# Strassen's seven products for the up projection of a hybrid decoder trunk, with block sums of its weights made by GpSimd

## The chip, the core and the metric

The kernel runs on one core of a Trainium2 chip. The metric is device time in microseconds (us) of one execution. Engines: TensorE (PE: matmuls, PEld: its weight loads), VectorE (DVE), ScalarE (ACT), GpSimd (POOL) and SyncE (SP, which issues most DMAs). Every engine runs its own instructions strictly in the order in which they stand in its queue.

## The reference

One layer on 2048 prompt tokens and 8 × 8 sample tokens, in float32, width 1024:

```python
h = rmsnorm(x, norm1_g)
q, ka, va, rw, gates = split(h @ w_in)              # 1024 x 4608
att = windowed_attention(q, ka, va, ...)
rw_out = rwkv7_mixer(rw, ...)
g_a, g_b = split(sigmoid(gates))
x = x + (g_a * (att @ w_pa) + g_b * (rw_out @ w_pb)) @ w_o
# conv_ffn(rmsnorm(x, norm2_g)):
ug, uv = split(h2 @ w_up)                           # 1024 x 2 * 2816
c = conv_b + sum_j conv_w[j] * shift(ug, j)         # causal, width 3
x = x + (gelu(c) * uv) @ w_down                     # 2816 x 1024
y = rmsnorm(x, final_g)
```

## The kernel before

Every large product takes three matmuls for each tile of 128 rows of the contraction: weights and activations are split into a high part (ACT rounds, `whi`, `A`/`B` first tile) and a low part (a subtraction, `wlo`), and hi·hi, hi·lo, lo·hi are added in PSUM. Activations lie with features on the partitions and tokens along the free axis.

**Phase 1** has six groups of 256 to 384 tokens. Each multiplies by the 36 tiles of `w_in` (1024 x 128 each) while attention and RWKV work of the same and of the previous group runs between the products; the order on PE is written out by hand (`ordered`, with the times `Y_...` at which each piece is taken). The rows of a raw product go through ACT into `raw`; POOL copies its last column into `carry` for the next group (line 624), and POOL also does `BK` (982, 983), `sp` (1166), `Y` (1274) and the scaling by the norm (532, 539). In the first three groups 72 weight tiles are split; their parts are written to memory and read back by the other groups.

**Phase 2** has three groups of 704 tokens, held as two halves of 352: `w_ab` (8 tiles of 1024 x 128), `w_o` (8), then the 22 f tiles of the up product, each once for `w_ug` and once for `w_uv`, in four parts of 6, 6, 6 and 4 f tiles, each part followed by its share of `w_down` (8 tiles). A weight tile of 8 x 128 columns serves 48 matmuls of 352 columns. It is split in two halves of 512 columns; `W_POOL = (2, 0)` gives every second half's subtraction to POOL, the other to DVE (`wsub`, line 424). The norm's factor `rs` isn't in the operand of the up product: the operand is x2 times the weight vector (line 1323, `A`), and `rs` is multiplied in where the products leave PSUM (1427) and on POOL (1449). So the up products need not wait for the norm. Behind each up product stand the width-3 convolution (1431, 1437), GELU (1445 to 1448) and, when the gate product is there, 1456 and the split of the result into `B` (1323).

## Time and profile before

| | |
|---|---|
| median of 3 runs | 3415.2 us (3404.68 to 3422.92) |
| profiled execution | 3414.19 us, span 3412.4 us |
| granted clock, mean | 0.975 |
| busy: PE | 3274.9 us (96%), 23574 matmuls |
| busy: DVE | 1941.7 us (57%) |
| busy: ACT | 1162.7 us (34%) |
| busy: POOL | 1106.6 us (32%) |

Busy time counts an engine's own instructions; neighbouring ones overlap a little, so the duration of one is longer than its share of a dense stretch. Phase 1 ends at about 1465 us.

### The profile page before, as it was taken

How to read it: one execution, taken by the hardware profiler on the slowest of the kernel's cores; microseconds unless marked ns; L12 is line 12 of the kernel's file. 1: busy time of each engine (PE TensorE's matmuls, PEld its weight loads, DVE VectorE, ACT ScalarE, POOL GpSimd, SP SyncE). 2: the span in 40 equal slices, each digit the busy share in tenths (PEclk: the TensorE clock that was granted, in tenths of full speed). 3: DMA queues.
4: the chain of work that ended last, by engine and by line, in shares of the span. 5: the costliest groups of instructions: out<-in, count | busy, mean ns of one | idle time of the engine just before them, and what ended most of it. 6: DMA issues, size and time to landing. Idle time of an engine off the chain costs nothing.

```text
span 3412.4 us, 59346 instructions
## 1 busy us (share of the span) xinstructions
PE 3274.9 (96%) x23574; PEld 3124.1 (92%) x23574; DVE 1941.7 (57%) x3658; ACT 1162.7 (34%) x2370; POOL 1106.6 (32%) x1242
## 2 busy tenths in 40 slices
PE   7899999989999999899999999999999999999998
PEld 6879888878888889799999999999999999999998
DVE  6764775664664765655454465555464655564564
ACT  4444443332333333223232233332232323232232
POOL 4333432321221222152233332423243342343342
PEclk9989989899999999999999999999999999999999
DMA  5446467684565658562222224512222352222222
GB/s 174 147 142 228 162 204 240 214 267 151 195 197 191 211 181 287 170 217 68 64 70 72 67 63 130 172 59 77 70 66 72 97 181 74 63 70 73 68 69 74
DMA packets 197069, 460.22 MB, mean 135 GB/s; under 512 B 62719, under 2 KB 95111, under 8 KB 196791
## 3 DMA queue, kind: packets, MB, share of 16 engines
q1 hardware_dynamic: 169367, 396.33, 36.0%
q0 software_dynamic: 8704, 37.78, 3.3%
q10 hardware_dynamic: 18720, 22.31, 1.8%
q8 instruction: 185, 3.03, 0.4%
...
HBM read 377.03 MB, written 79.31 MB: 134 GB/s over the span
## 4 chain that ended last, share of the span: by engine, by line
PE 78%; DVE 9%; DMA 6%; ACT 3%; issue 2%; POOL 2%; SPq 0%; ACTq 0%; DVEq 0%; POOLq 0%
PE acc L287 69%; PE ps L287 5%; DMA w<-w_in 2%; PE psA L287 2%; DVE LN L1034 1%; DVE TX L1032 1%; POOL wlo L424 1%; ACT whi L383 1%; PE psY L287 1%; ACT at L778 1%; DMA gates<-raw 1%; POOL th L1386 1%; DVE wlo L424 1%; DVE at L768 0%; DMA raw<-x 0%
## 5 line engine op out<-in xcount | busy, mean ns | idle before, releaser
L287 PE MATMUL acc<-A,whi 128*128 128x352 f32 x4992 | 1008.6, 323 | 3.8 <-DVE A L1320 3.1
L287 PE MATMUL acc<-h,whi 128*128 128x384 f32 (+2 forms) x3456 | 899.2, 340 | 14.3 <-DVE h L588 4.1
L287 PEld LDWEIGHTS acc<-A,whi 128*128 128x128 f32 x4992 | 837.3, 188 | 5.4 <-DVE A L1320 4.0
L424 POOL TENSOR_TENSOR wlo<-w,whi 128x512 fp32r<-128x512 f32 (+2 forms) x347 | 477.2, 1376 | 1070.4 <-ACT whi L383 977.9
L383 ACT CAST whi<-w 128x512 fp32r<-128x512 f32 (+2 forms) x696 | 373.6, 581 | 1066.9 <-PE acc L287 496.9
L287 PEld LDWEIGHTS acc<-h,whi 128*128 128x128 f32 x3456 | 621.8, 194 | 47.0 <-issue 15.1
L287 PE MATMUL acc<-A,wlo 128*128 128x352 f32 x2496 | 605.7, 324 | 0.0
L287 PE MATMUL acc<-B,whi 128*128 128x352 f32 x2880 | 582.5, 323 | 4.6 <-ACT B L1322 2.4
L287 PE MATMUL acc<-h,wlo 128*128 128x384 f32 (+2 forms) x1728 | 581.0, 336 | 1.4 <-DMA wlo<-w_in_lo 1.0
L287 PEld LDWEIGHTS acc<-B,whi 128*128 128x128 f32 x2880 | 481.9, 188 | 6.4 <-DVE B L1323 3.3
L424 DVE TENSOR_TENSOR wlo<-w,whi 128x512 fp32r<-128x512 f32 (+2 forms) x349 | 302.8, 868 | 256.8 <-ACT whi L383 244.4
L287 PEld LDWEIGHTS acc<-A,wlo 128*128 128x128 f32 x2496 | 435.4, 188 | 0.1
L287 PE MATMUL acc<-B,wlo 128*128 128x352 f32 x1440 | 350.2, 323 | 0.0
L287 PEld LDWEIGHTS acc<-h,wlo 128*128 128x128 f32 x1728 | 334.3, 193 | 15.0 <-issue 3.6
L287 PEld LDWEIGHTS acc<-B,wlo 128*128 128x128 f32 x1440 | 250.9, 188 | 0.0
L1478 DVE TENSOR_TENSOR x<-x,acc 128x352 f32<-128x352 f32 x188 | 89.3, 516 | 227.2 <-PE acc L287 227.2
L1449 POOL TENSOR_TENSOR ss<-ss,ssq 128x704 f32<-128x704 f32 x66 | 113.2, 1715 | 297.2 <-DVE ss L1448 264.0
L1437 DVE SCALAR_TENSOR_TENSOR cc<-ub,vt,cc 128x704 f32<-128x704 f32 (+1 forms) x132 | 145.9, 1105 | 37.4 <-ACT cc L1431 35.6
L1427 DVE TENSOR_TENSOR ub<-acc,ssq 128x352 f32<-128x352 f32 (+1 forms) x132 | 61.5, 507 | 117.5 <-PE acc L287 116.2
L1323 DVE SCALAR_TENSOR_TENSOR B<-ss,B 128x704 fp32r<-128x704 f32 x66 | 113.4, 1718 | 4.0 <-ACT B L1322 3.9
L1445 ACT ACTIVATE ss<-cc 128x704 f32<-128x704 f32 x66 | 52.4, 793 | 162.4 <-DVE cc L1437 110.5
L619 ACT COPY raw<-acc 128x384 f32<-128x384 f32 (+1 forms) x84 | 37.4, 445 | 168.4 <-PE acc L287 164.1
...
## 6 DMA issues: line engine op xcount, KB each, us to landing
whi<-w_in_hi SPq DMA_DIRECT2D x144, 512.0 KB, 4.6
wlo<-w_in_lo SPq DMA_DIRECT2D x144, 512.0 KB, 3.9
w<-w_in SPq DMA_DIRECT2D x72, 512.0 KB, 4.5
w<-w_ug SPq DMA_DIRECT2D x66, 512.0 KB, 3.5
w<-w_uv SPq DMA_DIRECT2D x66, 512.0 KB, 3.5
...
w_in_hi<-whi SPq DMA_DIRECT2D x36, 512.0 KB, 2.7
w_in_lo<-wlo SPq DMA_DIRECT2D x36, 512.0 KB, 5.3
```

The costliest lines, as they stand in the source:

```text
L287: self.pe(self.nc.tensor.matmul(out, lhsT, rhs, start=start, stop=stop), max(n * (1 if rhs.dtype == F32R else 4) / 2.4, 25))
L383: nc.scalar.copy(out=hi[:, a:b], in_=w[:, a:b])
L424: i = eng.tensor_tensor(**kw)
L619: nc.scalar.copy(out=raw[:, 1:1 + n], in_=acc[:, :n])
L778: nc.scalar.activation(out=t[:, h, :], in_=t[:, h, :], func=AF.Exp, bias=nm[:, h:h + 1], accum_out=su[:, h:h + 1])
L1032: nc.vector.tensor_tensor(out=tv, in0=LN[:NL, j:j + 1, j + 1:32].broadcast_to([NL, j, w]), in1=LN[:NL, 0:j, j:j + 1].broadcast_to([NL, j, ...
L1323: nc.vector.scalar_tensor_tensor(out=lo[:, :T], in0=src[:, :T], scalar=scale, in1=hi[:, :T].bitcast(F32), op0=MUL, op1=SUB)
L1427: nc.vector.tensor_tensor(out=ub[:, 2 + a:2 + e], in0=pp[:, :e - a], in1=rs[:, a:e], op=MUL)
L1437: nc.vector.scalar_tensor_tensor(out=cc[:, :n], in0=ub[:, j:j + n], scalar=self.v(wn, f), in1=cc[:, :n], op0=MUL, op1=ADD)
L1445: nc.scalar.activation(out=s[:, :T], in_=cc[:, :T], func=AF.Square, scale=GELU_A)
L1449: nc.gpsimd.tensor_tensor(out=s[:, :T], in0=s[:, :T], in1=rs[:, :T], op=MUL)
L1478: nc.vector.tensor_tensor(out=x2[m][:, a:b], in0=x2[m][:, a:b], in1=pp[:, :b - a], op=ADD)
```

## The change

**Up product.** Tokens are taken as two halves and the contraction as two halves of 512, and two neighbouring f tiles as the two halves of the output: a 2 x 2 by 2 x 2 block product in seven block products (Winograd's form) instead of eight. A run is one pair of f tiles of `w_ug` or of `w_uv`; a block product is 4 x 128 rows by 128 columns by 352 tokens, 12 matmuls. Two block products share one weight tile ("chunk", 24 matmuls). The results are combined as they leave PSUM (`product`: line 1473 `u`, 1476 `u3`, 1466; `put` of the up run, 1646, and of the gate run, 1662 and 1663).

**Operands.** The norm is now multiplied into x2 before the up product (`scaled`, line 1564); four sums of activation blocks are made (`second_chunk`, 1680 to 1690) and all seven operands are split (1334). `w_o` is run once for each token half, so its tiles are loaded and split twice; the norm of the first half is made inside the second run of `w_o`. In the first part of a group the block products 1 and 2 of all six runs stand ahead of the others; they need only the first half's operands.

**Weight sums.** Four sums of the four blocks of each weight pair are made once, on POOL, by `weight_sums`, spawned in phase 1: 88 times two loads of 128 KB, four subtractions or additions of 128x128 and one store of 256 KB, 23 MB read and 23 MB written in all. Two buffers `ws` serve it.

**Weights of phase 2** come as one stream in the order of use: loaded three tiles ahead and split one ahead (`next_w2`), with seven slots for raw, high and low tiles. `W_POOL` is set so that every subtraction of a split is DVE's, in phase 1 too. Outside a stretch from the end of `w_o` to the tenth chunk, PE's order in phase 2 is no longer written by hand.

```diff
-W_POOL = (2, 0)
+W_POOL = (1 << 30, 0)
...
+            self.sums_d = [[self.dram.tile([128, 4, 4, 128], F32, name=f"sums{x}{i}") for i in range(cfg.ff // 2)] for x in "gv"]
...
+            self.spawn(self.weight_sums())
...
-            self.bufs = dict(A=16, B=16, x2=8, th=4, tm=2, ub=2, cc=2, ss=2, ssq=1, carry=2, nrm=3)
+            self.bufs = dict(A=56, B=12, x2=8, th=4, ub=2, cc=2, ss=4, u=6, u3=1, ug=1, ssq=1, carry=2, nrm=3)
...
+            self.ordered = False
+            self.worder2, self.at2, self.nload2, self.nsplit2, self.raw2, self.split2 = self.weight_order(), 0, 0, 0, [], []
...
+    def weight_sums(self):
+        nc = self.nc
+        yield Y_weight_sums_1
+        last = None
+        for i in range(self.cfg.ff // 2):
+            for x, wn in enumerate(("w_ug", "w_uv")):
+                for k in range(4):
+                    v = self.t("ws", [128, 4, 128])
+                    for j in range(2):
+                        nc.gpsimd.dma_start(out=v[:, 2 * j:2 * j + 2], in_=self.A[wn][2 * i + j][:, k::4])
+                    if last:
+                        nc.gpsimd.dma_start(out=last[0], in_=last[1])
+                    yield Y_weight_sums_2
+                    a11, a12, a21, a22 = (v[:, j] for j in range(4))
+                    for o, p, q, op in ((a22, a21, a22, ADD), (a21, a11, a21, SUB), (a11, a22, a11, SUB), (a12, a12, a11, SUB)):
+                        nc.gpsimd.tensor_tensor(out=o, in0=p, in1=q, op=op)
+                    last = self.sums_d[x][i][:, :, k], v
+                    yield Y_weight_sums_2
+        nc.gpsimd.dma_start(out=last[0], in_=last[1])
...
+    REST = (6, 7, 5, 4, 3)
+    def part_chunks(self, part):
+        runs = [(0, part[0] // 2)]
+        for i, f in enumerate(part):
+            runs += [(0, u // 2) for u in part[i + 1:i + 2]] + [(1, f // 2)]
+        if part[0] == 0:
+            seq = [(*r, p) for r in runs for p in (1, 2)] + [(*r, p) for r in runs for p in self.REST]
+        else:
+            seq = [(*r, p) for r in runs for p in (1, 2) + self.REST]
+        return runs, [seq[i:i + 2] for i in range(0, len(seq), 2)]
...
+    def next_w2(self, *what):
+        order = self.worder2
+        while self.nload2 < min(self.at2 + 4, len(order)):
+            spec = order[self.nload2]
+            w = self.wtile("w", F32)
+            if isinstance(spec[0], str):
+                name, m, a, b = spec
+                kt = b - a
+                self.nc.sync.dma_start(out=w[:, :kt], in_=self.A[name][m][:, a:b])
+            else:
+                kt = 4 * len(spec)
+                for j, (x, i, p) in enumerate(spec):
+                    self.nc.sync.dma_start(out=w[:, j * 4:j * 4 + 4], in_=self.block_src(x, i, self.PRODUCTS[p][1]))
+            self.raw2.append((w, kt, None))
+            self.nload2 += 1
+        while self.nsplit2 < min(self.at2 + 2, len(order)):
+            self.split2.append(self.split_w(self.raw2.pop(0)))
+            self.nsplit2 += 1
+        assert order[self.at2] == what, (order[self.at2], what)
+        self.at2 += 1
+        return self.split2.pop(0)
...
+    def block_product(self, wt, k0, xs):
+        (hi, lo), w, o = wt, self.cfg.tmax2 // 2, self.pt("acc")[:, :self.cfg.tmax2 // 2]
+        for k in range(4):
+            xh, xl = xs[k]
+            for i in range(3):
+                self.mm(o, (hi, hi, lo)[i][:, k0 + k, :], (xh, xl, xh)[i], k == 0 and i == 0, k == 3 and i == 2)
+        return o
+    PRODUCTS = {1: ("b11", "a11"), 2: ("b21", "a12"), 3: ("b22", "s4"), 4: ("t4", "a22"), 5: ("t1", "s1"), 6: ("t2", "s2"), 7: ("t3", "s3")}
...
+    def product(self, R, p, wt, k0):
+        nc, w = self.nc, self.cfg.tmax2 // 2
+        o = self.block_product(wt, k0, R.ops[self.PRODUCTS[p][0]])
+        def five():
+            R.put(1, 1, R.u3, R.p5)
+            nc.vector.tensor_tensor(out=R.u, in0=R.p5, in1=R.u, op=ADD)
+        if p == 1:
+            R.u = self.t("u", [128, w])
+            nc.scalar.copy(out=R.u, in_=o)
+        elif p == 2:
+            R.put(0, 0, R.u, o)
+        elif p == 6:
+            nc.vector.tensor_tensor(out=R.u, in0=o, in1=R.u, op=ADD)
+        elif p == 7:
+            R.u3 = self.t("u3", [128, w])
+            nc.vector.tensor_tensor(out=R.u3, in0=o, in1=R.u, op=ADD)
+            if R.p5 is not None:
+                five()
+        elif p == 5:
+            R.p5 = o
+            if R.u3 is not None:
+                five()
+        elif p == 4:
+            R.put(1, 0, R.u3, o)
+        else:
+            R.put(0, 1, R.u, o)
+    def run_products(self, chunk, runs):
+        wt = self.next_w2(*chunk)
+        for k, (x, i, p) in enumerate(chunk):
+            R = runs[x, i]
+            if p > 2 and R.hold:
+                R.hold = False
+                for z in R.held:
+                    R.put(*z)
+            self.product(R, p, wt, k * 4)
 
...
-            h2.append(self.split(x, "A", T, self.v("n2", m)))
...
+        def norm(c):
+            (a, b), more = chunks[c], [lastsq]
+            yield from self.rstd_steps(rs[:, a:b], b - a, "acc", more)
+        def scaled(dst, m, c):
+            a, b = chunks[c]
+            nc.vector.scalar_tensor_tensor(out=dst, in0=x2[m][:, a:b], scalar=self.v("n2", m), in1=rs[:, a:b], op0=MUL, op1=MUL)
+        def first_chunk():
+            for j in range(4):
+                h = self.t("ss", [128, TM])
+                h1.append(h)
+                for i, n in ((0, "b11"), (1, "b21")):
+                    d = h[:, i * w:i * w + w]
+                    scaled(d, i * 4 + j, 0)
+                    ops[n][j] = self.split_half(d)
+        for c, (a, b) in enumerate(chunks):
+            for m in range(8):
+                hi, lo = self.next_w2("w_o", m, 0, 8)
+                if c == 1 and m == 7:
+                    self.ordered, self.last_pe = True, None
+                pp, = self.gemm2(hi, lo, mix, (c,))
+                x = x2[m]
+                if c == 0:
+                    nc.gpsimd.dma_start(out=x[:, :T], in_=A["x"][m][:, c0:c1])
+                nc.vector.scalar_tensor_tensor(out=x[:, a:b], in0=pp[:, :w], scalar=0.5, in1=x[:, a:b], op0=MUL, op1=ADD)
+                if m < 7:
+                    self.sumsq(rs, x, m, a, b)
+                else:
+                    lastsq = self.t("cc", [128, TM])[:, a:b]
+                    nc.scalar.activation(out=lastsq, in_=x[:, a:b], func=AF.Square)
+                if c == 1 and m == 1:
+                    for _ in norm(0):
+                        pass
+                    first_chunk()
+        norm1 = norm(1)
...
-            nc.gpsimd.tensor_tensor(out=s[:, :T], in0=s[:, :T], in1=rs[:, :T], op=MUL)
...
+        def gate(f, ss, acts):
+            done, out = [0, 0], [None, None]
+            def put(row, c, s, ps):
+                a, b = chunks[c]
+                x = ss[row][:, a:b]
+                t = self.t("ug", [128, w])
+                nc.vector.tensor_tensor(out=t, in0=ps, in1=s, op=ADD)
+                nc.vector.tensor_tensor(out=x, in0=x, in1=t, op=MUL)
+                done[row] += 1
+                if done[row] == 2:
+                    out[row] = self.split(ss[row], "B", T)
+                    if None not in out:
+                        acts.extend(lambda c, h=h: [z[:, c * w:c * w + w] for z in h] for h in out)
+            return Run(1, f // 2, put)
+        h2 = [None] * 4
+        def second_chunk(stage):
+            for j in range(4):
+                if stage == 0:
+                    h2[j] = self.t("th", [128, TM])
+                p, q, r, s = h1[j][:, :w], h1[j][:, w:T], h2[j][:, :w], h2[j][:, w:T]
+                if stage == 0:
+                    scaled(r, j, 1)
+                    nc.vector.tensor_tensor(out=p, in0=r, in1=p, op=SUB)
+                    ops["t1"][j] = self.split_half(p)
+                elif stage == 1:
+                    scaled(s, 4 + j, 1)
+                    nc.vector.tensor_tensor(out=p, in0=s, in1=p, op=SUB)
+                    ops["t2"][j] = self.split_half(p)
+                elif stage == 2:
+                    nc.vector.tensor_tensor(out=r, in0=s, in1=r, op=SUB)
+                    ops["t3"][j] = self.split_half(r)
+                elif stage == 3:
+                    nc.vector.tensor_tensor(out=q, in0=q, in1=p, op=SUB)
+                    ops["t4"][j] = self.split_half(q)
+                else:
+                    ops["b22"][j] = self.split_half(s)
 
...
+            order, todo = self.part_chunks(part)
+            runs = {}
             for f in part:
-                s = up(f)
-                if pend is not None:
-                    acts.append(gate(*pend))
-                pend = (f, s)
-            acts.append(gate(*pend))
+                runs[0, f // 2], o = up(f)
+                runs[1, f // 2] = gate(f, o, acts)
+            if part[0] == 0:
+                for r in order[1:]:
+                    runs[r].hold = True
+            for i, chunk in enumerate(todo):
+                if part[0] == 0:
+                    if i in (1, 2):
+                        next(norm1, None)
+                    if 2 <= i < 7:
+                        second_chunk(i - 2)
+                    if i == 9:
+                        self.ordered = False
+                self.run_products(chunk, runs)
...
```

Counts by the code: the up product has 44 tiles x 48 = 2112 matmuls in a group before, and 11 pairs x 2 runs x 7 x 12 = 1848 after. Tiles split in a group of phase 2: 92 before, 8 + 16 + 77 + 32 = 133 after.

On POOL's queue, in phase 1's first group, before: one subtraction of a weight split between the copies that end a raw tile (`raw`, `carry`).

```order
L624 COPY carry_233<-raw_768 128x1
L424 TENSOR_TENSOR wlo_780<-w_775,whi_779 128x512
L621 MEMSET raw_929 128x1
L624 COPY carry_233<-raw_833 128x1
L424 TENSOR_TENSOR wlo_843<-w_840,whi_842 128x512
L952 COPY PC_443<-t_P_878 128x6
L983 TENSOR_TENSOR BK_910<-xk_772,t_sw_874 64x6x64 x2
L621 MEMSET raw_971 128x1
```

After, at the same place in the first group:

```order
L1385 TENSOR_TENSOR ws_4592<-ws_4592 128x128 x4
L1379 DMA ws_4723<-w_ug 128x2x128 x2
L1381 DMA sumsg2_104<-ws_4592 512x1x128
L627 COPY carry_255<-raw_855 128x1
L624 MEMSET raw_951 128x1
L1385 TENSOR_TENSOR ws_4723<-ws_4723 128x128 x4
L1379 DMA ws_4901<-w_ug 128x2x128 x2
L1381 DMA sumsg2_104<-ws_4723 512x1x128
L956 COPY PC_465<-t_P_900 128x6
```

The splits are gone from POOL, and weight sums stand between the same copies. Read along the whole queue, 25 of the 88 stores of sums stand ahead of the fourteenth `COPY carry` of the first group (the last raw tile of its RWKV rows), 57 ahead of its first `Y`, and all 88 ahead of the second tile's `BK` of the second group.

On DVE's queue, at the norm of a group's second half (before: the norm of the whole group, ahead of the first up results, first token group), before:

```order
L436 SCALAR_TENSOR_TENSOR nrm_17366<-nrm_17366,nrm_17364 128x6
L437 SCALAR_TENSOR_TENSOR nrm_17365<-nrm_17366,nrm_17365 128x6
L452 MEMSET nrm_21924 128x1
L424 TENSOR_TENSOR wlo_17572<-w_17569,whi_17571 128x512
L1427 TENSOR_TENSOR ub_17417<-acc_17334,ssq_16772 128x352
L1427 TENSOR_TENSOR ub_17417<-acc_17335,ssq_16772 128x352
L1437 SCALAR_TENSOR_TENSOR cc_17418<-ub_17417,vt_90,cc_17418 128x704 x2
L1446 SCALAR_TENSOR_TENSOR ss_17426<-ss_17426,cc_17418 128x704
L1448 SCALAR_TENSOR_TENSOR ss_17426<-ss_17426,cc_17418 128x704
```

After, where the second half's norm is in (second token group; `wlo_24718` is the low part of the chunk that PE takes next):

```order
L426 TENSOR_TENSOR wlo_24718<-w_24582,whi_24717 128x512 x2
L1564 SCALAR_TENSOR_TENSOR th_24686<-x2_23904,vt_90,ssq_23903 128x352
L1564 SCALAR_TENSOR_TENSOR th_24693<-x2_23905,vt_90,ssq_23903 128x352
L1680 TENSOR_TENSOR ss_24313<-th_24686,ss_24313 128x352
L1680 TENSOR_TENSOR ss_24324<-th_24693,ss_24324 128x352
L1564 SCALAR_TENSOR_TENSOR th_24700<-x2_23906,vt_90,ssq_23903 128x352
L1334 TENSOR_TENSOR A_24690<-ss_24313,A_24689 128x352
L1680 TENSOR_TENSOR ss_24335<-th_24700,ss_24335 128x352
L1334 TENSOR_TENSOR A_24697<-ss_24324,A_24696 128x352
L1564 SCALAR_TENSOR_TENSOR th_24707<-x2_23907,vt_90,ssq_23903 128x352
L1564 SCALAR_TENSOR_TENSOR th_24686<-x2_23908,vt_90,ssq_23903 128x352
L1334 TENSOR_TENSOR A_24704<-ss_24335,A_24703 128x352
```

Before, a split and the first results follow the norm at once. After, 21 instructions of 352 columns (12 of them shown) stand between the split of one chunk (`wlo_24718`) and that of the next (`wlo_24779`).

On DVE's queue among the up products, before (one f tile of up and one of gate):

```order
L1427 TENSOR_TENSOR ub_17627<-acc_17577,ssq_16772 128x352
L1427 TENSOR_TENSOR ub_17627<-acc_17578,ssq_16772 128x352
L424 TENSOR_TENSOR wlo_17782<-w_17779,whi_17781 128x512
L1437 SCALAR_TENSOR_TENSOR cc_17628<-ub_17627,vt_90,cc_17628 128x704 x2
L1446 SCALAR_TENSOR_TENSOR ss_17636<-ss_17636,cc_17628 128x704
L1448 SCALAR_TENSOR_TENSOR ss_17636<-ss_17636,cc_17628 128x704
L1456 TENSOR_TENSOR ss_17499<-ss_17499,acc_17650 128x352
L1456 TENSOR_TENSOR ss_17499<-ss_17499,acc_17651 128x352
L424 TENSOR_TENSOR wlo_17846<-w_17843,whi_17845 128x512
L1323 SCALAR_TENSOR_TENSOR B_17703<-ss_17499,B_17702 128x704
```

After, a place in the first part of the second token group (two chunks):

```order
L426 TENSOR_TENSOR wlo_24984<-w_24889,whi_24983 128x512 x2
L1646 TENSOR_TENSOR ub_25002<-acc_24989,u3_24978 128x352
L1466 TENSOR_TENSOR u_24604<-acc_24989,u_24604 128x352
L1662 TENSOR_TENSOR ug_25188<-acc_24738,u_24736 128x352
L1646 TENSOR_TENSOR ub_25002<-acc_25005,u3_24978 128x352
L426 TENSOR_TENSOR wlo_25034<-w_24942,whi_25033 128x512 x2
L1623 SCALAR_TENSOR_TENSOR cc_25019<-ub_25002,vt_90,cc_25019 128x704
L1646 TENSOR_TENSOR ub_24619<-acc_25039,u_24604 128x352
L1623 SCALAR_TENSOR_TENSOR cc_25019<-ub_25002,vt_90,cc_25019 128x704
L1646 TENSOR_TENSOR ub_25064<-acc_24668,u_24666 128x352
L1623 SCALAR_TENSOR_TENSOR cc_25053<-ub_24619,vt_90,cc_25053 128x704
L1632 SCALAR_TENSOR_TENSOR ss_25025<-ss_25025,cc_25019 128x704
```

Before, one half of a split stands among four or five instructions; after, both halves (`x2`), and each block product that leaves PSUM brings one addition or two, ahead of the same convolution and GELU (1623, 1632).

## Rows read from the trace of the kernel before

**Rows 1.** Busy time of each engine in phase 1 and phase 2 (stretches; x: instructions that started).

```profile
core 0: us, PE busy (x) PEld busy (x) DVE busy (x) ACT busy (x) POOL busy (x), PEclk, DMA share, GB/s
0.00:1465.00 1465.00, 1354.91 (x11631) 1208.38 (x11632) 905.10 (x2165) 562.28 (x1407) 435.60 (x611) 0.95 0.60 198
1465.00:3412.00 1947.00, 1919.96 (x11945) 1915.73 (x11944) 1036.59 (x1494) 600.41 (x964) 671.01 (x631) 0.99 0.28 87
```

**Rows 2.** What PE waited for in phase 2: total us, times, longest.

```profile
PE acc L287 <- DVE ssq L1333: 7.0, 2, 3.8
PE acc L287 <- DVE nrm L437: 5.4, 1, 5.4
...
```

**Rows 3.** PE in phase 1, one stream into one bank: start, us, instruction.

```profile
1080.08 0.52 PE L287 MATMUL acc<-h,whi 128*128 128x384 f32 x2
...
1080.61 0.52 PE L287 MATMUL acc<-h,whi 128*128 128x384 f32 x2
```

**Rows 4.** DVE's groups in phase 2 by shape: busy us, mean ns, idle before.

```profile
L424 DVE TENSOR_TENSOR wlo<-w,whi 128x512 fp32r<-128x512 f32 x178 | 178.1, 1001 | 110.9 <-ACT whi L383 110.4
...
L1437 DVE SCALAR_TENSOR_TENSOR cc<-ub,vt,cc 128x704 f32<-128x704 f32 x88 | 99.0, 1125 | 26.4 <-ACT cc L1431 24.9
...
L1456 DVE TENSOR_TENSOR ss<-ss,acc 128x352 f32<-128x352 f32 x132 | 62.5, 516 | 34.6 <-PE acc L287 34.6
L1446 DVE SCALAR_TENSOR_TENSOR ss<-ss,cc 128x704 f32<-128x704 f32 x66 | 58.9, 893 | 60.2 <-ACT ss L1445 60.2
```

**Rows 5.** Single lines on DVE: ns min/median/max, first and last start.

```profile
L424 DVE TENSOR_TENSOR wlo<-w,whi x349: 424/692/2669, 16.3 to 3375.7; 128x512 fp32r<-128x512 f32 x127, 128x384 fp32r<-128x384 f32 x36, 128x256 fp32r<-128x256 f32 x12
...
L1437 DVE SCALAR_TENSOR_TENSOR cc<-ub,vt,cc x132: 871/952/1983, 1598.7 to 3333.8; 128x704 f32<-128x704 f32 x88, 128x640 f32<-128x640 f32 x44
...
L1323 DVE SCALAR_TENSOR_TENSOR B<-ss,B x66: 876/1973/1982, 1615.3 to 3348.0; 128x704 fp32r<-128x704 f32 x66
```

**Rows 6.** DVE in phase 2: two neighbours as one piece (start, us).

```profile
1651.09 0.95 DVE L1456 TENSOR_TENSOR ss<-ss,acc 128x352 f32<-128x352 f32 x2 [4.58 <-PE acc L287]
```

**Rows 7.** A step of the norm, DVE, 1560 to 1600 us.

```profile
L437 DVE SCALAR_TENSOR_TENSOR nrm<-nrm 128x6 f32<-128x6 f32 x3 | 0.5, 167 | 0.1
```

**Rows 8.** All engines in the first 349 us, in four stretches (columns as in rows 1).

```profile
0.00:127.00 127.00, 98.39 (x555) 86.11 (x556) 83.88 (x134) 56.65 (x109) 53.56 (x80) 0.96 0.46 154
127.00:237.00 110.00, 98.35 (x869) 89.26 (x869) 76.34 (x196) 51.69 (x134) 40.64 (x35) 0.90 0.55 174
...
sum 349.00, PE 306.85 PEld 275.72 DVE 219.65 ACT 157.50 POOL 134.82; mean PE 76.71 PEld 68.93 DVE 54.91 ACT 39.38 POOL 33.71
```

**Rows 9.** Line 424 on POOL in the same stretches.

```profile
0.00:127.00 127.00, 24.19 (x16) 0.96 0.46 154
...
sum 349.00, POOL 64.62; mean POOL 16.16
```

**Rows 10.** POOL's groups in phase 1 by shape: busy us, mean ns.

```profile
L424 POOL TENSOR_TENSOR wlo<-w,whi 128x512 fp32r<-128x512 f32 x73 | 104.5, 1432 | 206.2 <-ACT whi L383 171.2 <-ACT vt L723 14.4 <-DMA w_in_lo<-wlo 10.4
...
L1274 POOL TENSOR_TENSOR Y<-Y,gr 128x512 f32<-128x512 f32 x16 | 17.2, 1074 | 46.9 <-DVE gr L437 41.0 <-DVE nrm L437 5.8
...
L539 POOL TENSOR_TENSOR at<-at,rstd 128x256 f32<-128x256 f32 x2 | 1.4, 730 | 2.0 <-DMA at<-x 2.0
...
L1192 POOL DMA_DIRECT2D BK<-state_wkv x2 | 1.1, 568 | 11.0 <-PE ps L290 11.0
...
L1274 POOL TENSOR_TENSOR Y<-Y,gr 128x256 f32<-128x256 f32 x1 | 0.6, 613 | 6.0 <-DVE gr L437 6.0
```

**Rows 11.** DMA issues in 0 to 488 us: KB each, median us to landing.

```profile
w<-w_in SPq DMA_DIRECT2D x59, 512.0 KB, 4.4
...
PTm<-sel POOLq DMA_DIRECT2D x1, 256.0 KB, 5.9
...
bias_d<-at POOLq DMA_DIRECT2D x1, 8.0 KB, 2.7
```

**Rows 12.** The chain that ended last, 0 to 488 us, shares by line.

```profile
by line: PE acc L287 27.0%; DMA w<-w_in 14.4%; PE ps L287 6.1%; issue 3.9%; POOL wlo L424 3.6%; ACT whi L383 3.6%; PE psA L287 3.4%; DVE LN L1034 3.1%; DVE TX L1032 2.8%; DVE wlo L424 2.3%; ACT at L778 1.8%; DMA LN<-ln 1.3%; DVE at L768 1.3
```

More of the change, by code (lines that the diff above doesn't have):

```diff
@@ new lines, in block_src, with parts @@
+    def block_src(self, x, i, what):
+        ap = self.A["w_ug" if x == 0 else "w_uv"]
+        if what[0] == "s":
+            return self.sums_d[x][i][:, "2431".index(what[1])]
+        return ap[2 * i + int(what[1]) - 1][:, int(what[2]) * 4 - 4:int(what[2]) * 4]
+    REST = (6, 7, 5, 4, 3)
+    def parts(self):
+        ff = self.cfg.ff
+        return [list(range(f, min(f + 6, ff), 2)) for f in range(0, ff, 6)]
+    def part_chunks(self, part):
[7 more added lines that the diff above has]
+        return runs, [seq[i:i + 2] for i in range(0, len(seq), 2)]
@@ new lines, in weight_order @@
+    def weight_order(self):
+        order = []
+        for _ in self.cfg.groups2:
+            order += [("w_ab", m, 0, 8) for m in range(8)] + [("w_o", m, 0, 8) for _ in range(2) for m in range(8)]
+            for part in self.parts():
+                order += [tuple(c) for c in self.part_chunks(part)[1]]
+                order += [("w_down", m, part[0], part[0] + 2 * len(part)) for m in range(8)]
+        return order
+    def next_w2(self, *what):
[19 more added lines that the diff above has]
+        return self.split2.pop(0)
@@ L1368, in group2 @@
         chunks = [(i * w, (i + 1) * w if i < nchk - 1 else T) for i in range(nchk)]
+        assert nchk == 2 and w * 2 == T == TM
         if g == 0:
@@ L1386, in group2 @@
             nc.gpsimd.tensor_tensor(out=ta[:, :T], in0=ta[:, :T], in1=tb[:, :T], op=ADD)
-            mix.append(self.split(ta, "B", T, 0.5))
-        if g:
-            self.drain(done)
-        x2, h2 = [], []
-        rs = self.t("ssq", [128, TM])
-        for m in range(8):
-            hi, lo = self.weights("w_o", m)
-            ps = self.gemm(hi, lo, mix, 0, chunks, "acc")
-            x = self.t("x2", [128, TM])
-            nc.gpsimd.dma_start(out=x[:, :T], in_=A["x"][m][:, c0:c1])
-            for (a, b), pp in zip(chunks, ps):
-                nc.vector.tensor_tensor(out=x[:, a:b], in0=x[:, a:b], in1=pp[:, :b - a], op=ADD)
-            h2.append(self.split(x, "A", T, self.v("n2", m)))
-            self.sumsq(rs, x, m, T)
-            x2.append(x)
@@ L1403, in group2 @@
-        norm = self.spawn(self.later(L_SSQ, self.rstd_steps(rs, T, "acc")))
+            if m < 6:
+                h = self.split(ta, "B", T)
+                mix.append(lambda c, h=h: [x[:, c * w:c * w + w] for x in h])
+            else:
+                h = [self.split_half(ta[:, a:b]) for a, b in chunks]
+                mix.append(lambda c, h=h: h[c])
+            if m:
+                next(done, None)
+        rs = self.t("ssq", [128, TM])
+        x2 = [self.t("x2", [128, TM]) for _ in range(8)]
@@ L1448, in up @@
             nc.vector.scalar_tensor_tensor(out=s[:, :T], in0=s[:, :T], scalar=1.0, in1=cc[:, :T], op0=ADD, op1=MUL)
[L1449 removed]
             return s
[L1452 to L1457 removed]
+        def up(f):
+            ub, done, out = [None, None], [0, 0], [None, None]
+            def put(row, c, s, ps):
+                if ub[row] is None:
+                    ub[row] = self.t("ub", [128, TM + 18])
+                u, (a, b) = ub[row], chunks[c]
+                e = min(b, n)
+                nc.vector.tensor_tensor(out=u[:, 2 + a:2 + e], in0=ps[:, :e - a], in1=s[:, :e - a], op=ADD)
+                if b > n:
+                    uv = u[:, 2 + n:2 + n + 80].rearrange("p (s t) -> p s t", t=10)
+                    nc.vector.tensor_tensor(out=uv[:, :, 2:10], in0=by8(ps[:, n - a:b - a]), in1=by8(s[:, n - a:b - a]), op=ADD)
+                done[row] += 1
+                if done[row] == 2:
+                    out[row] = conv(f + row, u)
+            return Run(0, f // 2, put), out
```

127 lines of the change are left out of this document (68 added, 59 removed).

## The prediction

> **What bounds the kernel now.** I first read the busy time of each engine in the two phases [rows 1]. In phase 2 PE is busy for 1919.96 of 1947 us. Every microsecond of PE work taken away there is gained if the other engines keep up, and DVE (1036.59 us) looks as if it had room. In phase 1 PE is busy for 1354.91 of 1465 us, and the next engine is DVE with 905.10. Next come PE's waits in phase 2 [rows 2]: the norm between sum of squares and first up result (7.0 and 5.4 us) is nearly all that is named, and some 20 us in all come back with any version. So phase 2 is PE-bound. Phase 1's first groups are a chain of several engines: in 0 to 488 us the chain [rows 12] gives PE's two largest lines 27.0% and 6.1%, the loads of `w_in` 14.4% (70 us), POOL's subtractions 3.6% (17.6 us).
>
> **The products.** In phase 2 a matmul costs 1919.96 us / 11945 = 160.7 ns [rows 1]. The up product loses 2112 − 1848 = 264 matmuls in each of three groups, 792 in all: 792 x 0.1607 = 127.3 us off PE. The new products write one bank in a row instead of alternating between two. Phase 1 already does that with 384 columns: three in 0.53 us, 177 ns [rows 3], 0.46 ns a column as with 352 in phase 2. So the new form isn't slower on PE. A chunk of 24 matmuls takes 3.86 us.
>
> **What DVE must do in a chunk.** Before, one 512-column half of a split for 48 matmuls; after, two halves for 24. A half takes 0.692 us where nothing disturbs it (median), 1.001 on average in phase 2 [rows 4, 5]. A pair of f tiles, up and gate, is 7 chunks and 27.0 us of PE. DVE then has 14 halves x 0.69 = 9.7 us; 18 instructions of 352 columns (7 of the up run, 11 of the gate run) x 0.516 = 9.3; four convolution steps x 0.871 and four GELU steps x 0.893 = 7.1; two splits of the result, now without the factor, x 0.88 = 1.8 [rows 4, 5]. That is 27.8 us, with some 1.5 us of small instructions 29.3: more than PE. But neighbours overlap: two of 0.516 us take 0.95 us together [rows 6], 0.08 us less, and 42 of them give back 3.4 us: 25.9 us. DVE is at 96% of PE in the up stage if every neighbour overlaps, at 108% if none does; an instruction that needs its predecessor's result may not overlap, which no row here prices.
>
> These durations are those without POOL beside them. Line 1323 shows what POOL does to DVE: 0.876 us at the least, 1.973 as a median, with POOL subtracting or multiplying at the same time [rows 5]. After, POOL has neither in phase 2, so I take the low ends. The Trainium skill, GPSIMD Engine Reference, section "Key points", says that GpSimd shares its SBUF interfaces with VectorE and that DVE instructions with two SBUF inputs suffer from it; this trace agrees (factor 2.25). With the means instead (1.001 and 1.125) a pair would cost DVE 14 x 0.31 + 4 x 0.25 = 5.3 us more, and DVE would be the bound.
>
> **New stalls in phase 2.** The split of a chunk can begin only when PE has left the chunk two before, whose slots it takes. A chunk has then 3.86 us for ACT's and DVE's 2 us: some 2.3 us of DVE's other work fit ahead of a split before PE waits.
> - Norm of the first half, inside `w_o`: between two splits stand nine steps of 0.167 us [rows 7] and 17 instructions at 0.435, 8.9 us; with the split's 1.4 that is 10.3 against 3.86 + 2.3. 4.2 us a group, 13 in all.
> - Second half's operands: 21 instructions x 0.435 = 9.1 us between two splits as shown in the order, so 4.4 to 4.7 us a group, 14 in all.
> - Rest of the first part: DVE has 66 us by the prices above (held results of products 1 and 2 come out here too) against 58 of PE: between 0 and 9.6 us a group. I take 5, 15 in all.
> - Later parts: convolution and GELU of two f tiles come together and delay one split by some 2.4 us a pair; part of it is slack. Between 0 and 10 us a group; 10 in all.
> - The third group's sample columns double some additions: 6.
>
> Together 58 us; between 15 (overlap everywhere) and 134 (no overlap: 33 pairs x 2.3 us more). The 16 tiles of `w_o` instead of 8 cost PE nothing, since each has 24 matmuls. Loads rise by 41 tiles of 512 KB a group over a DMA share of 0.28 [rows 1]: nothing. POOL's multiplication by `rs` (line 1449) was off PE's path: nothing.
>
> **Weight sums on POOL.** No row has a 128x128 instruction with two inputs. 128x512 took 1.432 (with DVE beside it) or 1.074, 128x256 0.730 or 0.613 [rows 10]; the step is 0.46 to 0.70 for 256 columns, so 128 come to 0.38 us either way. Four of them, each waiting for the one before, 1.7 us. A DMA issue takes 0.568 [rows 10]; three of them 1.7. So a sum costs POOL 3.4 us at the least, and 88 cost 299. POOL's other work in the first 349 us is 134.82 − 64.62 = 70.2 us [rows 8, 9]. By the order all sums are done where POOL stood at 349 us before, so POOL is late by at least 299 + 70 − 349 = 20 us, or 33, since in the first 127 us (25 sums, 85 us, plus 53.56 − 24.19 = 29.4) it still has 13 us free. Above that come waits for the DMAs in POOL's own queue: transfers issued by POOL landed after 2.7 us (8 KB) to 5.9 us (256 KB) [rows 11]. In the order shown (sum, load, store, sum) a sum waits for its load: 1.7 + 1.1 + 2.7 = 5.5 us each; where two are nested, 4.4. At 4.4, half of POOL's other work filling the waits, POOL is late by 387 + 35 − 349 = 73 us. Behind a sum in the queue stand `carry`, `raw`, `BK`, `sp` and `Y`, and for them DVE and PE wait in an order written by hand; so lateness on POOL goes to the end of phase 1, less some slack (PE is idle for 42 of these 349 us anyway [rows 8]). I take 46 us between 33 and 73. DVE instead of POOL for the splits halves 17.6 us of chain: −9. Reading and writing 46 MB beside 154 to 224 GB/s delays the loads of `w_in`: between 0 and a quarter of their 70 us, I take 8. Phase 1: +45, between 0 and +110. PE's granted clock was 0.90 in 127 to 237 us, where it waited most [rows 8]; more waiting can cost more there, which the upper bound holds.
>
> The Trainium skill, DMA: Bandwidth & Descriptors, section "Anatomy of one DMA — SWDGE (gpsimd) path", gives a DMA issued by GpSimd about 2.0 us that no size avoids, plus bytes over 436e3 per us: an estimate of 2.3 us for 128 KB. That speaks against sums with two buffers; the rows above are slower still, and by 2.3 a sum would cost 5.1 us in place of 5.5.
>
> **The sum.** 3414.2 (the profiled execution, 1 us below the median) − 127.3 + 58 + 45 = **3390 us**, 0.7% below the median. About 0.5% (17 us) is what a measurement of this kernel can tell from no change.
>
> **Rivals.**
> - *The sums are hidden.* POOL's lateness stays within buffers and within PE's idle time, phase 1 at 0: 3414 − 127 + 58 = 3345. For it: POOL is 32% busy. Against it: POOL must do at least 369 us of work in 349.
> - *The sums set the pace of groups 0 and 1* (slower). Waits for landing count in full, which the 5.9 us of [rows 11] makes possible: at 4.8 us a sum POOL is late by 422 + 35 − 349 = 108: 3414 − 127 + 58 + 105 = 3450. It decides from about 4.4 us a sum. For it: the order has sum, load, store again and again with two buffers.
> - *DVE bounds the up stage* (slower). No overlap: 3414 − 127 + 134 + 45 = 3466. For it: 96 to 108% above. Against it: its durations in quiet stretches.
> - *The products do not get cheaper*, as one bank holds PE up: 3414 + 58 + 45 = 3517 (slower). [rows 3] speaks against it.
>
> **How the numbers follow.** My forecast 0.36 (its own range 3360 to 3425: faster 0.22, same 0.13, slower 0.01). Sums hidden 0.26, all faster. Sums set the pace 0.23 (same 0.02, slower 0.21). DVE bound 0.12 (same 0.03, slower 0.09). Products not cheaper 0.03, slower. Faster 0.48, same 0.18, slower 0.34. The range leaves out one in ten on each side: 3315 (phase 2 with 30 us of stalls in a hidden phase 1) to 3475.
>
> **What would show it.** Right: about 792 fewer matmuls in phase 2 at 160 ns; phase 2 near 1878 us; PE waiting for DVE's `wlo` behind the norms; POOL without a pause in the first 350 us and phase 1 near 1510. `carry` copies, `BK` or `Y` as releasers of PE's or DVE's waits say that POOL is late; a phase 1 of 1465 says that it is hidden. Wrong if a sum on POOL takes under 3 us or over 4.5, or if PE waits for `wlo` in every chunk.

## The result, and the profile after

The changed kernel takes 3583.99 us (median; 3577.65 to 3589.03) against 3413.19 before: a ratio of 1.051, 95% interval 1.0474 to 1.0546. It is 5% slower; 3390 us was forecast, with a range to 3475. The first product of phase 2 (`w_ab`, the first matmul that reads `A`) cuts each profiled execution in two. One line of the tile `A` on PE, before and after, gives ns min/median/max and the first and last start:

```profile
L287 PE MATMUL acc<-A,whi x4992: 318/324/511, 1456.6 to 3345.5; 128*128 128x352 f32 x200
```

```profile
L289 PE MATMUL acc<-A,whi x4656: 317/323/634, 1673.9 to 3526.4; 128*128 128x352 f32 x194
```

Up to that matmul 1456.6 us before and 1673.9 after: +217.3. From there to the end of the span 1955.8 and 1905.7: −50.1. The sum, 167.2, is the difference of the spans (3579.6 − 3412.4). So the block products do save time, and phase 1 loses four times as much. (The rows ahead of the prediction and the expectations below cut the phases at 1465 and 1674 us; their loss of phase 1 is 209 us.)

The page of the changed kernel, busy tenths in 40 slices of 89.5 us:

```profile
PE   5764666999999999998999999999999999999998
...
DVE  5542525756646747566686865868686686868667
...
POOL 7778865223213212222110100121010012001100
PEclk8776787999999999998999999999999999999998
```

In the first five slices POOL stands at 7 to 8 tenths and PE at 4 to 7; before, PE stood at 7 to 9 in the first seven. The granted clock is 0.6 to 0.8 in these seven, where it was 0.8 to 0.9. For the same 11599 matmuls of phase 1 PE is idle for 294 us instead of 108 and busy for 1379.67 instead of 1348.62, at a mean granted clock of 0.89 instead of 0.95: 186 and 31 of the 217 us. The same shows in stretches (columns as in [rows 1]):

```profile
0.00:1674.00 1674.00, 1379.77 (x11599) 1227.84 (x11599) 929.42 (x2229) 555.19 (x1399) 696.89 (x1149) 0.89 0.61 201
1674.00:3580.00 1906.00, 1831.18 (x11222) 1805.51 (x11220) 1390.56 (x2593) 779.87 (x1397) 213.37 (x296) 0.98 0.39 123
0.00:560.00 560.00, 341.71 (x2319) 302.83 (x2320) 243.99 (x499) 156.81 (x354) 417.32 (x696) 0.78 0.57 186
```

In the first 560 us POOL is busy for 417 (its DMA issues count here) and PE for 342; before, 211 and 504. What PE waited for in that stretch (total us, times, longest):

```profile
PE ps L289 <- POOL BK L986: 48.8, 8, 14.5
PE acc L289 <- ACT raw L700: 38.0, 1, 38.0
PE acc L289 <- DVE wlo L426: 22.4, 1, 22.4
PE psY L289 <- POOL sp L1170: 21.1, 4, 8.4
PE ps L289 <- ACT TX L1067: 19.4, 2, 18.8
PE ps L289 <- POOL Y L1278: 14.2, 1, 14.2
```

`BK`, `sp` and `Y` are POOL's: 84 us; before, PE waited 1.2 us for `BK` in this stretch and for no `sp` or `Y`. DVE waited for POOL's writes to `raw` too, 86 us in all, and before for none; the two largest:

```profile
DVE xr L637 <- POOL raw L626: 29.6, 1, 29.6
DVE xk L637 <- POOL raw L624: 23.1, 4, 9.0
```

Here is why POOL is late, POOL's row of time from 121 us (start, length, in brackets the idle time before and its releaser):

```profile
121.57 0.74 POOL L1379 DMA_DIRECT2D ws<-w_ug  x1
122.31 0.77 POOL L1381 DMA_DIRECT2D sumsv<-ws  x1
123.12 0.18 POOL L627 COPY carry<-raw 128x1 f32<-128x1 f32 x1
123.25 0.09 POOL L624 MEMSET raw<- 128x1 f32 x1
125.17 2.05 POOL L1385 TENSOR_TENSOR ws<-ws 128x128 f32<-128x128 f32 x4 [1.83 <-DMA ws<-w_ug]
127.43 1.44 POOL L1379 DMA_DIRECT2D ws<-w_ug  x2 [0.22 <-issue]
128.87 0.77 POOL L1381 DMA_DIRECT2D sumsg<-ws  x1
131.07 3.32 POOL L1385 TENSOR_TENSOR ws<-ws 128x128 f32<-128x128 f32 x4 [1.44 <-DMA ws<-w_ug]
```

Sum follows sum, these two each with a wait for its own load. In all, 33 additions wait for a load and 36 load issues wait for a store that frees a buffer. The two lines of the sums on POOL, in ns (min/median/max), and what POOL waited for at the first and at the loads (us, times):

```profile
L1385 POOL TENSOR_TENSOR ws<-ws x352: 442/457/1961, 11.0 to 585.9; 128x128 f32<-128x128 f32 x176
...
  DMA ws<-w_uv: 22.1, 16
  DMA ws<-w_ug: 17.2, 17
...
L1379 POOL DMA_DIRECT2D ws<-w_ug x88: 702/720/775, 4.6 to 553.6; - x88
...
  DMA sumsg<-ws: 32.6, 18
  DMA sumsv<-ws: 24.9, 18
...
DMA to landing us min/median/max: 2.5/3.1/8.0
```

The page gives the 352 additions 189.0 us (538 ns on average). With 176 load issues at 0.72 (127 us), 88 stores at 0.75 (66 us) and the waits (96.8 us here, and 23.1 at the stores for the addition ahead of them) a sum takes POOL 502 / 88 = 5.7 us. The last ends at 586 us. Before, POOL reached that place at 349: it is 237 us late. The first `Y` (line 1274 before, 1278 now) moved from 237.3 to 383.7 us.

Phase 2's main new wait is DVE's (PE's waits from 1674 us on):

```profile
PE acc L289 <- DVE wlo L426: 33.8, 25, 3.4
PE acc L289 <- DVE nrm L454: 11.0, 3, 3.7
PE acc L289 <- DVE u L1473: 6.3, 4, 2.3
PE acc L289 <- DVE nrm L439: 5.6, 1, 5.6
```

792 matmuls at 160.7 ns would leave 1955.8 − 127.3 = 1828.5 us; measured 1905.7. New stalls are 77 us. Part of them are waits with a name (64 us in all, 21 before), part a slower pace: 1831.18 us for 11222 matmuls are 163.2 ns each. Most of them stand in one place, the first part of a group. First that of the first group, then its second part:

```profile
1808.70:1910.20 101.50, 90.22 (x531) 87.58 (x531) 91.73 (x176) 52.56 (x92) 13.29 (x16) 0.95 0.39 120
1956.20:2039.80 83.60, 82.19 (x506) 80.87 (x505) 73.55 (x124) 42.82 (x71) 10.43 (x12) 1.00 0.38 123
```

At 160.7 ns, 531 matmuls need 85.3 us and 506 need 81.3. In the first part DVE is busy for 91.7 us, more than the products need. The three first parts take 304 us, the nine later ones 670.

### The profile page after: what moved, and what is told of

It is laid out like the page before. It is cut to its first block, busy times and chain, and to the rows that moved or that the text cites. A ratio compares the mean times of both kernels' runs of the same rounds, so it can differ in the third digit from the quotient of the medians.

```text
span 3579.6 us, 60192 instructions
## 1 busy us (share of the span) xinstructions
PE 3210.9 (90%) x22818; PEld 3033.3 (85%) x22818; DVE 2320.0 (65%) x4821; ACT 1335.1 (37%) x2796; POOL 910.3 (25%) x1445
## 5 line engine op out<-in xcount | busy, mean ns | idle before, releaser
L289 PE MATMUL acc<-A,whi 128*128 128x352 f32 x4656 | 1099.8, 325 | 14.3 <-DVE u L1473 6.3
L385 ACT CAST whi<-w 128x512 fp32r<-128x512 f32 (+2 forms) x942 | 516.6, 590 | 963.7 <-PE acc L289 637.6
L289 PE MATMUL acc<-A,wlo 128*128 128x352 f32 x2328 | 724.2, 327 | 34.0 <-DVE wlo L426 32.9
L426 DVE TENSOR_TENSOR wlo<-w,whi 128x512 fp32r<-128x512 f32 (+2 forms) x942 | 626.9, 691 | 116.0 <-ACT whi L385 97.9
L1727 DVE SCALAR_TENSOR_TENSOR x<-acc,x 128x352 f32<-128x352 f32 x188 | 90.1, 519 | 271.3 <-PE acc L289 271.1
L1385 POOL TENSOR_TENSOR ws<-ws 128x128 f32<-128x128 f32 x352 | 189.0, 538 | 59.3 <-DMA ws<-w_uv 22.1
L289 PE MATMUL ps<-RA,BK 64*128 64x128 f32 (+1 forms) x592 | 62.9, 319 | 70.1 <-POOL BK L986 65.4
L1623 DVE SCALAR_TENSOR_TENSOR cc<-ub,vt,cc 128x704 f32<-128x704 f32 (+1 forms) x132 | 118.2, 924 | 11.3 <-ACT cc L1617 10.7
L289 PEld LDWEIGHTS ps<-RA,BK 64*128 64x128 f32 (+1 forms) x592 | 50.7, 215 | 83.5 <-POOL BK L986 68.5
L1646 DVE TENSOR_TENSOR ub<-acc,u 128x352 f32<-128x352 f32 (+1 forms) x132 | 66.6, 507 | 40.2 <-PE acc L289 37.7
```

The lines of the kernel that those rows point to most:

```text
L289: self.pe(self.nc.tensor.matmul(out, lhsT, rhs, start=start, stop=stop), max(n * (1 if rhs.dtype == F32R else 4) / 2.4, 25))
L385: nc.scalar.copy(out=hi[:, a:b], in_=w[:, a:b])
L426: i = eng.tensor_tensor(**kw)
L1385: nc.gpsimd.tensor_tensor(out=o, in0=p, in1=q, op=op)
L1623: nc.vector.scalar_tensor_tensor(out=cc[:, :n], in0=ub[:, j:j + n], scalar=self.v(wn, f), in1=cc[:, :n], op0=MUL, op1=ADD)
L1646: nc.vector.tensor_tensor(out=u[:, 2 + a:2 + e], in0=ps[:, :e - a], in1=s[:, :e - a], op=ADD)
```

## The experiments

Theory A: POOL's queue, full of weight sums, holds up phase 1. Rivals: B, the splits moved from POOL to DVE; C, the DMA traffic of the sums. For phase 2, theory D: DVE's load in the up stage; rival: only the two bursts at the norms.

**Without the sums.** The spawn is removed; phase 2 reads raw blocks of the weights instead of sums.

```diff
-            self.spawn(self.weight_sums())
-            return self.sums_d[x][i][:, "2431".index(what[1])]
+            return ap[2 * i][:, 0:4]
```

> The changed kernel without the weight sums (phase 2 reads raw weight blocks in their place, so the up product is not the reference's; loads, splits and matmuls of phase 2 stay as they are). Theory A (POOL's queue, full of sums, holds up phase 1): phase 1 ends near where it did before, 1465 us plus or minus 15 instead of 1674, and the whole is 3580 - 209 = 3370, about 1.2% faster than before. Rival B (the weight splits moved from POOL to DVE hold up the first groups): phase 1 still ends after 1600, the whole is above 3500. Rival C (DMA traffic of the sums) expects the same as A here and parts from it in the next run.

3341.21 us, ratio 0.9797 (0.9771 to 0.9823). B is out, and the loss goes with the sums: phase 1 ends 242 us earlier than with them. It is 25 us shorter than before, more than A said:

```profile
L289 PE MATMUL acc<-A,whi x4656: 317/323/509, 1431.8 to 3283.8; 128*128 128x352 f32 x194
```

**The traffic alone.** As above, but `weight_sums` is:

```diff
+                    for j in range(2):
+                        self.behind_pe(nc.sync.dma_start(out=self.sums_d[x][i][:, 2 * j:2 * j + 2, k], in_=self.A[wn][2 * i + j][:, k::4]))
+                    yield 4000
```

> As the run without sums, but the same bytes move in the first 350 us or so: 176 copies of 128 KB from the weights straight to the place of the sums, in pieces of 512 bytes, issued by SyncE 4 us apart; POOL does nothing for it. Theory A: within 15 us of the run without sums, phase 1 at most 1480. Rival C (46 MB read and written beside the loads of w_in make the first groups late): phase 1 well above 1550, most of the 209 us.

3350.09 us, ratio 0.9821 (0.9785 to 0.9856); phase 1 ends at 1443.3. The copies were issued from 38 to 476 us, so the traffic was denser than that of the sums (225 GB/s in the first 560 us, 186 in the changed kernel). The bytes cost 8.9 us by the medians and 11.5 in phase 1 of the profiled executions, not 209. C is out as the main cause. (`behind_pe` keeps an instruction in the queue order behind the PE instruction issued last; see the next edit.)

**The sums in their places.** Each load, addition and store of `weight_sums` goes through

```diff
+    def behind_pe(self, i):
+        if self.last_pe is not None:
+            self.tc.add_manual_dep(i.ins, self.last_pe, ORDER, reason="issue order")
```

> The changed kernel, but each load, addition and store of a weight sum is kept in program order behind the PE instruction issued last when it was written, so that the 88 sums lie 12 us apart from 120 us on in place of one behind the other from the start; nothing else changes. Theory A: no DMA wait stands in POOL's queue any more, POOL is held 2.2 us at a time; phase 1 ends at 1465 to 1520, the whole is 3375 to 3425. Rival C: the same bytes over 1050 us in place of 580 still cost some 100 us of phase 1. Rival B: no gain.

3376.19 us, ratio 0.9896 (0.9874 to 0.9917): the same work on the same engine, 208 us less than the changed kernel and 1.0% faster than before. Phase 1 ends at 1469.4. This shows A: what costs the time is where the sums stand in POOL's queue. Nor is it that POOL's additions slow DVE, since they are all still in phase 1 (DVE is busy there for 944 us, 929 in the changed kernel). One thing of the expectation was wrong: POOL still waits for the loads, some 100 us in all at its additions, but now between other work, over 1240 us:

```profile
L1389 POOL TENSOR_TENSOR ws<-ws x352: 446/459/2052, 185.7 to 1424.8; 128x128 f32<-128x128 f32 x176
...
  DMA ws<-w_uv: 63.3, 22
  DMA ws<-w_ug: 37.0, 15
```

**Phase 1's split halves back on POOL** (`W_POOL = (2, 0)` in the changed kernel).

> The changed kernel with phase 1's 72 halves of splits given back to POOL. Theory A: 65 of them, 1.4 us each, come on top of POOL's queue in the first groups: phase 1 later by 60 to 100 us, the whole 3640 to 3680. Rival B (DVE overloaded by the splits): faster than the changed kernel, 3500 or less.

3601.23 us, ratio 1.0557 (1.0522 to 1.0592): slower as A said and B did not, but by 17 us, not 60 to 100. The trace shows why: only 46 of the 72 halves, 60 us, run ahead of the end of the sums, and they fill waits that POOL had anyway (for a `ws` buffer, 25.1 us in place of 57.5). The last addition starts at 605.2 us in place of 585.9, 19 us later, and phase 1 ends 18 us later (1692.2).

**The same without sums:** no sums, halves on POOL.

> The run without sums, with phase 1's 72 halves of splits given back to POOL. Phase 1 without sums ended 25 us earlier than before. If that is what moving the splits to DVE gives: 1455 to 1465 again, the whole 3360 to 3375. If it has another cause, phase 1 stays at 1432.

3356.91 us, ratio 0.9844 (0.9822 to 0.9867), 16 us above the run without sums; in the profiled executions, of which this one lay 9 us above its median, the first `w_ab` matmul is at 1454.4 against 1431.8. So moving the splits to DVE is what shortened phase 1, by some 16 to 23 us.

**Issues by SyncE.** In the spaced kernel the loads and stores are `nc.sync.dma_start`.

> As the spaced run, but the loads and stores of the weight sums are issued by SyncE; POOL only does the four additions of each. In the changed kernel's trace a sum takes POOL 2 x 0.72 + 0.75 for the issues and some 2.15 for the additions; without the issues POOL has 88 x 2.2 = 190 us less to do. Theory A (time in POOL's queue is the cost): phase 1 falls from 1469 us towards the 1443 of the run with the traffic alone, 1440 to 1460; the whole 3345 to 3365. Rival (what is left of the 37 us between the spaced run and the run without sums is traffic or DVE being slowed by POOL's additions): no gain, 3376.

3383.61 us, ratio 0.9922 (0.9905 to 0.9939); phase 1 ends at 1472.3. No gain: less time in POOL's queue gave nothing here. But PE's wait for `wlo<-w_in_lo`, a load that SyncE issues too, grew from 5.9 to 12.1 us, so something was given back there, and the run doesn't show that POOL's time is free once the sums are spaced. Of the 38 us of phase 1 between spaced sums and none, some 10 are traffic; the rest stays open. The rival has a number: the 2229 instructions of DVE in phase 1 are busy for 913 us without sums, 916 with the traffic alone, 944 with spaced sums and 941 here. That PE loses by it wasn't tried.

**The two bursts cut.** On top of that, in phase 2:

```diff
-                    first_chunk()
+                if c == 1 and 1 <= m < 5:
+                    first_chunk(m - 1)
...
-                        second_chunk(i - 2)
...
                 self.run_products(chunk, runs)
+                if part[0] == 0 and 2 <= i < 7:
+                    second_chunk(i - 2)
```

with the operands' instructions kept behind the last PE instruction or the last split.

> As the run with SyncE's issues, with the two bursts on DVE cut in phase 2: the first half's operands are made two tiles at a time behind four products of w_o in place of eight behind one, and each stage of the second half's operands stands behind the next chunk's split. The prediction put 4.2 and 4.7 us a group on the two: phase 2 from 1905 to about 1880, the whole 25 us less than the run before it. Rival (the new stalls of phase 2 come from the up stage's load on DVE throughout): less than 8 us.

3374.34 us, ratio 0.9887 (0.9869 to 0.9904): 9 us less by the medians. But in the profiled executions phase 2 takes 1905.1 us, as in the run before it (1905.8); what differs there is phase 1 (1467.9 against 1472.3). PE's waits for `wlo` fell from 35.1 to 26.5 us and came back elsewhere. So the 25 us aren't there, and the rival's "less than 8" is what phase 2 shows. The work is the same, and in the first part of a group, where the second burst stands, DVE has no room to spread it into (columns as in [rows 1]):

```profile
1602.30:1702.60 100.30, 90.25 (x530) 86.20 (x530) 91.40 (x176) 52.68 (x92) 11.58 (x16) 0.97 0.38 121
```

**A lighter DVE.** The SyncE version without the two GELU multiplications (1632 and 1634) of each f tile, so GELU isn't computed.

> As the run with SyncE's issues, with two of DVE's instructions for each f tile left out, the multiplications by the gate branch in GELU (0.89 us each, 132 of them, 118 us of DVE in phase 2; outputs differ). Theory D (DVE bounds the up stage or comes close): phase 2 shorter by 30 to 80 us. Rival (DVE has room there, and only the norms stall): less than 15 us.

3321.33 us, ratio 0.9739 (0.9721 to 0.9758); phase 2 takes 1853.3 us, 52.5 less for 118 us less on DVE (by the medians the whole is 62 less). D holds. In the changed kernel DVE sat idle for 0.2 us in all ahead of these 132 instructions, so what they cost is DVE's work and not a wait for ScalarE. The up stage loses by DVE throughout, but not evenly: the three first parts of the groups go from 304.3 to 273.9 us, the nine later ones from 669.7 to 648.4.

**Work from DVE to POOL.** First every fourth half of the up stage's splits (`self.pool_every = 4` around `next_w2` in `run_products`), then line 1663 as `nc.gpsimd.tensor_tensor`, both on the version with the bursts cut.

> As the run with the bursts cut (3374 us), with every fourth half of the up stage's splits given to POOL, which is nearly idle there: 115 halves, 80 us less on DVE. Leaving out 118 us of DVE's work made phase 2 shorter by 52. Theory D (DVE's load in the up stage is what PE waits for) without contention: 35 us faster, 3340. Rival (POOL slows DVE's instructions with two operands from SBUF, as it did before in line 1323, 1973 against 876 ns): POOL's 115 x 1.3 us give back as much as is won, 3365 to 3400.

> As the run with the bursts cut, with the last multiplication of the gate run (two operands from SBUF, 128x352) on POOL: 132 instructions, 68 us less on DVE. Theory D without contention: 30 us faster, 3345. Rival (contention): POOL needs about 0.9 us each, 119 us in which DVE goes slower; no gain or a loss.

3391.41 (0.9939; 0.9917 to 0.996) and 3405.04 us (0.9977; 0.9961 to 0.9993): 17 and 31 us slower than without. Phase 2 takes 1921.3 and 1938.5 us (the latter in an execution 8 us above the median). DVE's groups in phase 2, first with the bursts cut, then with POOL taking halves (busy us, mean ns):

```profile
L427 DVE TENSOR_TENSOR wlo<-w,whi 128x512 fp32r<-128x512 f32 x602 | 426.9, 731 | 11.4 <-ACT whi L386 9.9
...
L1644 DVE SCALAR_TENSOR_TENSOR ss<-ss,cc 128x704 f32<-128x704 f32 x66 | 57.5, 884 | 0.2
```

```profile
L427 DVE TENSOR_TENSOR wlo<-w,whi 128x512 fp32r<-128x512 f32 x493 | 372.5, 774 | 8.7 <-ACT whi L386 6.8 <-POOL wlo L427 1.2
...
L1646 DVE SCALAR_TENSOR_TENSOR ss<-ss,cc 128x704 f32<-128x704 f32 x66 | 68.4, 1041 | 0.0
```

The 109 fewer subtractions save 54 us on that line; the others take longer, the second GELU step (1644 and 1646 are the same step) 1041 instead of 884 ns. So DVE's busy time in phase 2 did not fall at all: 1390.0 us with the bursts cut, 1390.2 with the halves and 1387.9 with the multiplication on POOL. And POOL's half takes 1590 ns; PE waits for it 3 times, 5.7 us. The Trainium skill, GPSIMD Engine Reference, section "Key points", says that GpSimd shares its SBUF interfaces with VectorE and that DVE instructions with two SBUF inputs contend with it. The run agrees: `ug<-acc,u`, which reads one input from PSUM, kept its time (519 and 518 ns).

**Work from DVE to ScalarE.** GELU by ScalarE's table, one instruction in place of four, on the version with the bursts cut and on the spaced one; the factor 0.5 behind `w_down` goes.

```diff
-            nc.scalar.activation(out=s[:, :T], in_=cc[:, :T], func=AF.Square, scale=GELU_A)
-            nc.vector.scalar_tensor_tensor(out=s[:, :T], in0=s[:, :T], scalar=1.0, in1=cc[:, :T], op0=ADD, op1=MUL)
-            nc.scalar.activation(out=s[:, :T], in_=s[:, :T], func=AF.Tanh, scale=GELU_B)
-            nc.vector.scalar_tensor_tensor(out=s[:, :T], in0=s[:, :T], scalar=1.0, in1=cc[:, :T], op0=ADD, op1=MUL)
+            nc.scalar.activation(out=s[:, :T], in_=cc[:, :T], func=AF.Gelu_apprx_tanh)
```

> As the run with the bursts cut (3374 us), with GELU as one instruction on ScalarE (its table of GELU by tanh) in place of Square, a DVE step, Tanh and a DVE step: 118 us less on DVE, two ScalarE passes in place of... one instead of two. Theory D (DVE's load is what PE waits for in the up stage): as in the run that left the two DVE steps out, 50 us faster, 3315 to 3330. Rival (a table load at each change of function, or the chain's latency): no gain, or a loss.

> The spaced run (3376 us) with the same one edit and nothing else: the changed kernel with its sums put in their places and GELU on ScalarE. Theory D: 3315 to 3330, the same gain of some 50 us. Rival: none.

3314.7 us, ratio 0.9708 (0.9681 to 0.9735), and 3325.7, 0.9746 (0.9721 to 0.9772): 60 and 50 us below their bases, the fastest versions that compute the whole. DVE's other instructions keep their durations (a subtraction `wlo` of 128x512 takes 732 ns, 731 before). ScalarE loads a table once more, at 1643 us, and not at each change of function. Phase 2 takes 1846.0 us in the first, 17.5 above the 1828.5 of the products. Its waits of PE, from 1467 us on:

```profile
PE acc L290 <- DVE nrm L456: 11.4, 4, 3.7
PE acc L290 <- DVE wlo L427: 8.2, 10, 1.7
PE acc L290 <- DVE nrm L441: 5.6, 1, 5.6
```

The wait for `wlo`, 26.5 us with GELU's steps on DVE, is 8.2. A first and a second part of a group:

```profile
1599.90:1688.30 88.40, 85.51 (x531) 83.66 (x530) 81.22 (x163) 49.44 (x87) 8.35 (x16) 1.00 0.43 137
1734.70:1815.70 81.00, 81.00 (x507) 81.00 (x507) 65.17 (x112) 39.26 (x65) 5.10 (x12) 1.00 0.40 127
```

In the second run, whose bursts are not cut, phase 2 takes 1854.6 us, 8.6 more, and 7.3 of these lie in the three first parts. So cutting the bursts is worth something once DVE has room, and was worth 0.7 us before.

## Why the prediction was wrong

**The products** were right: 792 fewer matmuls, and a product into one bank runs at the old pace (median of a matmul 323 ns against 324, both by the same reckoning). The mean pace of phase 2, 163.2 ns against 160.7, is no sign of the rival "the products do not get cheaper": with GELU on ScalarE it is 161.1 (1808.94 us for 11228).

**New stalls in phase 2**: forecast 58 (15 to 134), measured 77. The size is near, but partly by luck, since its parts were not. The two bursts, 27 us in the sum, gave 0.7 us of phase 2 when they were cut. What costs the time is the sum of DVE's work in the up stage, which the prediction put at 25 us and kept as a rival: taking 118 us off DVE gave back 52 of the 77. It is dearest where the bursts and the products' results come together, in the first part of a group: DVE is busy for 91.7 us there and the products need 85.3, and the three first parts lose 48 us. In a later part of six f tiles DVE is busy for 73.6 us, some 90% of the 81.3 that the products need and below the forecast 96%, and PE still loses 2 to 3 us.

**Weight sums on POOL** is the step that failed: "I take 46 us between 33 and 73", and phase 1 "+45, between 0 and +110". Measured +217 for phase 1, and 242 between the changed kernel and the one without sums, some 10 of them traffic. The mechanism, the place and the waiting instructions were those named, and POOL's lateness, 237 us, did go to the end of phase 1 nearly whole; the size of that lateness was wrong. POOL's own time for a sum was put at 3.4 us from rows of other shapes; it is 2.15 for four additions (not 1.7) and 2.19 for three issues (not 1.7: 0.72 to 0.75 each, not 0.57), 4.3 in all. Waits add 1.4 (1.1 for loads and buffers, 0.3 for the addition ahead of a store), though the prediction had written that a sum which waits for its load takes 5.5, and then counted on nesting (4.4) and on other work filling the waits. With its own 5.5 the lateness comes to 88 x 5.5 + 70 − 349 = 205 us, and the whole to some 3549. And this price was left out of the bounds: the upper end was 110. Nor did that bound hold what the lower clock costs, as the prediction said it would: 31 us of phase 1 are longer busy time of PE at a granted clock of 0.89 instead of 0.95. The rival "the sums set the pace" said "from about 4.4 us a sum" and stood at 0.23; at 5.7 it decides. The prediction's own sign of being wrong, a sum over 4.5 us, is the one that came true.

**DVE for the splits in phase 1**: −9 forecast, −16 to −23 measured without sums. **DMA traffic**: +8 forecast, 9 to 11.5 measured.

Three readings of the prediction were off and change nothing in its sum. The norm's two waits are 12.4 of the 20.7 us that PE's waits in phase 2 name, not nearly all. PE waited most in the first 127 us (idle for 28.6, granted clock 0.96), not in 127 to 237 us (11.7, clock 0.90) [rows 8]. And POOL still multiplies in phase 2 (`th<-th`, 24 times 2.0 us), though not beside the up products.
